# A hybrid encoder layer with experts: the first norm's gain and bias applied to turned tokens, 16 products for the residual rows inside the query projections, another order of VectorE's work in the last routing, and another order of the first expert pair's fetches

## The chip, the cores and the metric

The kernel runs on one core of one Trainium2 chip. Its time is the device time of one execution in microseconds (us); a median over several executions stands for a kernel. A profiled execution also has a span, from the first to the last recorded instruction. PE is TensorE (matmuls), DVE is VectorE, ACT is ScalarE, POOL is GpSimd, and SP is SyncE, which here only starts transfers (DMAs). Each engine carries out its own instructions strictly in order and waits on semaphores for the others.

## The reference, cut to what matters

512 tokens of 1024 features go through a layer norm, two attentions that read one input projection, a second norm, and a layer of 32 experts of which each token uses two.

```
h  = layer_norm(x, ln_emb_g, ln_emb_b)            # (x - mean) * rsqrt(var + eps) * g + b
p  = h @ w_in                                     # queries and keys of A, low-rank q and kv of B
A  = windowed attention of 8 heads, B = latent attention (q = rms(q_a) @ w_q_b, kv = rms(kv_a) @ w_kv_b)
h2 = layer_norm(alpha * h + concat(rms(A), rms(B)) @ w_out, ln_attn_g, ln_attn_b)
expert group: top 1 of 4; inside it the top 2 of 8 experts
y[t] = sum over t's two experts of w * ((silu(h2 @ w_gate[e]) * (h2 @ w_up[e])) @ w_down[e])
out = layer_norm(alpha * h2 + y, ...)
```

The first norm's result h is used twice: turned (features on the partitions) as the projections' operand, and as token rows `z` that are added to the attention's output much later.

## The kernel before, in words

The tokens are four tiles of 128 (`NT` = 4), the features eight blocks of 128 (`NK` = 8). Products that need more than one pass of TensorE's fp32 arithmetic are split into a high and a low part, and `mm3` makes three matmuls of one (high by high, low by high, high by low: the three lines 213 to 215). `split` makes the two parts: a copy on ScalarE (line 208) and a difference on VectorE or, for the first weight chunk's `wl`, on GpSimd (line 209).

1. **First norm** (the loop at lines 246 to 262). For each tile the rows are loaded, normalised with gain and bias by VectorE (lines 203 and 204), turned by TensorE (line 257), and split into `hth` and `htl`. The gain and the bias stand as rows repeated on all partitions (`lng`, `lnb`, four loads of 256 KB), and `cst`, which has the unit matrix for the turning, is loaded behind them on SP's queue. The first weights of `w_in` follow.
2. **Projections** by chunks of `w_in`, then the small projections of attention B: `wprep` loads, scales and splits pieces of `w_kv_b` and `w_q_b` (lines 358 to 360), `heads` turns keys and queries (line 468), lines 445 and 447 turn attention A's queries, and line 484 writes the values `vb`.
3. **Attentions B and A**, then the output projection.
4. **Routing.** For each token tile the logits of 36 outputs, the top expert group, and a place for each (token, expert). The last two tiles are called `a` (tile 2) and `b` (tile 3). From here on the order of all engines is the order of the code, written out by hand; up to here a scheduler with a model of the engines' times sets the order of every engine.
5. **Experts**, 16 pairs. The rows of a pair's tokens come by an indirect load from `norm_rows` (`fetch`, on GpSimd's queue), except for pair 0, whose rows `xT0` are made by matmuls with a one-hot matrix `sel` (`gather`, line 1109). A pair is 32 gate and up matmuls (`gates`, line 1243), the SiLU on ScalarE (1247), the product `hid` on VectorE (1248), and 16 matmuls with `w_dn` (1263). The weights of three pairs stand in a ring of buffers, loaded by SP in order: 4 MB for gate and up and 2 MB for down of each pair. A buffer is loaded anew as soon as its last reader is done.

In `run_pair` for pair 0 the kernel before issues four gate matmuls, then the 16 small matmuls that give the places of the next tokens (line 1368), `places_rows` and `fetch` for them, the mixing `weights` of tiles 1 to 3, and then the remaining gate matmuls. The gate matmuls go through the feature blocks 0 to 7.

Of the kernel before, what the change touches and what calls it, by code (L numbers as in the profile page):

```python
# [12 lines left out]
F32 = mybir.dt.float32  # L13
# [4 lines left out]
AF = mybir.ActivationFunctionType  # L18
# [3 lines left out]
P = 128  # L22
# [49 lines left out]
def build(tc, A, out):  # L72
# [24 lines left out]
    with top:  # L97
# [38 lines left out]
        def bvec(pl, src, n, name):  # L136
            t = pl.tile([P, n], F32, name=name)
            SY.dma_start(out=t, in_=src.partition_broadcast(P))
            return t
        load_x(0)  # L140
        lg, lb = [lp.tile([P, D], F32, name=nm) for nm in ("lng", "lnb")]
        for n in range(2):
            for dst, nm in ((lg, "ln_emb_g"), (lb, "ln_emb_b")):
                SY.dma_start(out=dst[:, 512 * n:512 * n + 512], in_=A[nm][512 * n:512 * n + 512].partition_broadcast(P))
        SY.dma_start(out=cst, in_=A["cst"][:, :C_KEEP])

        nch = [-1]

        def chunk_load(pieces):
            nch[0] += 1  # L150

            n = sum(w for _, w in pieces)
            hs = []
            for q in range(4):
                if q == 1 and nch[0] == 0:
                    load_x(1)
                wf, wh, wl = [wp.tile([P, 2, 512], dt, name=nm, bufs=4)
                              for nm, dt in (("wf", F32), ("wh", F32R), ("wl", F32R))]
                o = 0
                for c0, w in pieces:  # L160
                    SY.dma_start(out=wf[:, :, o:o + w],
                                 in_=A["w_in"][0, 256 * q:256 * q + 256, c0:c0 + w]
                                 .rearrange("(k p) f -> p k f", p=P))
                    o += w
                split(wf[:, :, :n], wh[:, :, :n], wl[:, :, :n], PO if nch[0] == 0 else V)
                hs.append((wh, wl))
            return n, hs
# [21 lines left out]
        def ln_stats(src, eps=LN_EPS):  # L189
# [7 lines left out]
            return mv, rs  # L197

        def layer_norm(src, dst, g, b):
            mv, rs = ln_stats(src)  # L200
            for i in range(2):
                sl = slice(512 * i, 512 * i + 512)
                V.scalar_tensor_tensor(dst[:, sl], src[:, sl], mv[:, 0:1], g[:, sl], ALU.subtract, ALU.mult)
                V.scalar_tensor_tensor(dst[:, sl], dst[:, sl], rs, b[:, sl], ALU.mult, ALU.add)

# [42 lines left out]
        for t in range(NT):  # L248
            if t == 0:
                chunks.append(chunk_load([(768, 512)]))  # L250
            elif t + 1 < NT:
                load_x(t + 1)
            layer_norm(xs[t], z[t], lg, lb)
            for kk in range(2):
                pt = ptr()
                for k in range(4):
                    PE.transpose(pt[:, k * P:(k + 1) * P],
                                 z[t][:, (4 * kk + k) * P:(4 * kk + k + 1) * P], ident)
                pv = pt.rearrange("p (a b) -> p a b", a=4)
                o = (slice(None), slice(4 * kk, 4 * kk + 4), slice(t * P, (t + 1) * P))  # L260
                split(pv, hth[o], htl[o])
        lnst.close()
# [199 lines left out]
        w2 = pool(p2, "w2", side="right")  # L462
        scr = pool(p2, "p2s", bufs=2, side="right")

        def heads(src, hi, lo, c, t):
# [21 lines left out]
        for c in range(2):  # L487
            wh, wl = wprep(w2, A["w_q_b"][0], gq, 6, 384 * c, 384)
            for t in range(NT):
                ts_ = slice(t * P, (t + 1) * P)  # L490
                qt_ = scr.tile([P, 4, 96], F32, name="qtok")
                pp = pproj()
                for k in range(6):
                    mm3(pp[:, :384], cth[:, k, ts_], ctl[:, k, ts_], wh[:, k, :], wl[:, k, :],
                        k == 0, k == 5)
                pv = pp[:, :384].rearrange("p (a b) -> p a b", a=4)
                SC.mul(qt_[:, :, 0:64], pv[:, :, 0:64], rq[t][:, 0:1])
                rope(qt_[:, :, 64:96], pv[:, :, 64:96], tabb, t, 4, 16, scr, scale=rq[t][:, 0:1])
                heads(qt_, qth, qtl, c, t)
# [648 lines left out]
        rsqrt(rr, sp[0][:, 0:1], ALPHA ** 2 / 512, ALPHA ** 2 * RMS_EPS)  # L1148
        norm_bias(a, 0)
        logits(a, 0)  # L1150
        logits(a, 1)
# [10 lines left out]
        wout_l(1, p1_)  # L1162
        steps(route(a))
        place(1)
        turn(b, 0)
        count(a)
        add_z(1, p1_)
# [9 lines left out]
        turn(b, 1)  # L1177
        place(a)
        sel0_(1)
        sel0_(a)  # L1180
        logits(b, 0)
        logits(b, 1)
        offset(b)
        for i in (1, 0):
            scaled(b, i)
        norm_gain(a, 1)
        biased(b)
        norm_bias(a, 1)
        for i in range(2):
            keep(a, i)  # L1190
        gather(0, range(2))
        gather(1, range(2))
        steps(route(b))
        count(b)
        gather(a, [0])
        gain(b, 1, V)
        place(b)
        sel0_(b)
        gather(a, [1])
        gain(b, 0, V)  # L1200
        shift(b, 1, V)
        shift(b, 0, V)
# [36 lines left out]

        def gates(pg, xT, ws, j0, j1):  # L1240
            for j in range(j0, j1):
                for i in range(2):
                    PE.matmul(pg[64 * i:64 * i + 64], xT[:, j, 64 * i:64 * i + 64], ws[i][0][j], start=(j == 0), stop=(j == 7))  # L1243

# [116 lines left out]
        def run_pair(p, xT, meanwhile):  # L1361
            pg = new_gates()
            if p == 0:
                gates(pg, xT, ws[p], 0, 2)
                pi = psd("places")
                for t in range(NT):
                    for u in range(4):
                        PE.matmul(pi[:, 2 * u:2 * u + 2], (sel0[t], sels[1][t])[u // 2][:, P * (u % 2):P * (u % 2) + P],
                                  cmb[t][:, 2 * u:2 * u + 2, 0], start=(t == 0 and u == 0), stop=(t == NT - 1 and u == 3))
                for g in range(2):  # L1370
                    for u, pl in enumerate(places_rows(pi[:, 4 * g:4 * g + 4], 2, 2, 1)):
                        plc[2 * g + u] = pl
                        fetch(2 * g + u, pl)
                for t in range(1, NT):
                    weights(t)
                gates(pg, xT, ws[p], 2, 8)
            else:
                gates(pg, xT, ws[p], 0, 8)
            load_next(p)
# [4 lines left out]
        def residual(p):  # L1384

            SC.mul(plc[p]["xg"], plc[p]["xg"], plc[p]["of"])

        xT = xT0
# [54 lines left out]
        with tc.If(nmax > 0):  # L1443
            with tc.For_i(0, NP) as p_:
# [3 lines left out]
                with tc.For_i(0, more) as r_:  # L1448
# [19 lines left out]
                    pg = new_gates("pwo")  # L1468
                    gates(pg, xT2, w_, 0, 8)
                    leave_rows(gated(pg), w_, pl)  # L1470
# [16 lines left out]
        with tc.issue_after(last):  # L1487
            gates(pg, xT, ws[p], 0, 8)
        hT = gated(pg)
# [121 lines left out]
```

## Time and profile before

| what | value |
|---|---|
| median of 3 runs | 592.62 us (591.76 to 593.85) |
| the profiled execution's own time | 591.33 us |
| its span | 589.5 us |
| PE busy | 523.4 us (89%) |
| DVE busy | 322.6 us (55%) |
| ACT busy | 222.1 us (38%) |
| POOL busy | 99.9 us (17%) |
| moved by DMA | 141.76 MB, mean 240 GB/s |

The rows further below are of two kinds. A row of a timeline gives the start, the length, the engine, the line, the operation, what it writes and reads, how many alike stand in the row, and in brackets how long the engine had been idle before it and what ended that. Where a row stands for several instructions, they overlap a little, so that the distance of two starts is shorter than one's length. A row of windows gives the busy time of each engine in a stretch, the granted TensorE clock as a part of 2.4 GHz, the DMA engines' busy share, and the GB/s.

### The profile page before, as it was taken

How to read it: one execution, taken by the hardware profiler on the slowest of the kernel's cores; microseconds unless marked ns; L12 is line 12 of the kernel's file. 1: busy time of each engine (PE TensorE's matmuls, PEld its weight loads, DVE VectorE, ACT ScalarE, POOL GpSimd, SP SyncE). 2: the span in 40 equal slices, each digit the busy share in tenths (PEclk: the TensorE clock that was granted, in tenths of full speed). 3: DMA queues.
4: the chain of work that ended last, by engine and by line, in shares of the span. 5: the costliest groups of instructions: out<-in, count | busy, mean ns of one | idle time of the engine just before them, and what ended most of it. 6: DMA issues, size and time to landing. Idle time of an engine off the chain costs nothing. (4 is left out here: it accounts for less than half of the span.)

```text
span 589.5 us, 8004 instructions
## 1 busy us (share of the span) xinstructions
PE 523.4 (89%) x2756; PEld 331.8 (56%) x2757; DVE 322.6 (55%) x882; ACT 222.1 (38%) x477; POOL 99.9 (17%) x141
## 2 busy tenths in 40 slices
PE   2899999999898999999998899999998699979860
PEld 1688898789766777677777444343433234323230
DVE  4946463775688757947768734434524222202177
ACT  2256451564597738856731312111111111101032
POOL 1700221311100000213200201123111101000051
PEclk9999999999899999999999989999999889989985
DMA  8983310221201005991266799999999999999663
GB/s 279 280 290 81 102 43 0 59 81 42 85 16 58 1 1 212 289 367 39 66 258 259 280 391 410 420 415 415 411 417 400 421 418 391 412 420 416 264 267 142
DMA packets 46268, 141.76 MB, mean 240 GB/s; under 512 B 12380, under 2 KB 19420, under 8 KB 37009
## 3 DMA queue, kind: packets, MB, share of 16 engines
q1 hardware_dynamic: 40608, 131.06, 58.5%
q0 software_dynamic: 4464, 8.06, 3.6%
q10 hardware_dynamic: 1152, 2.10, 0.9%
q8 instruction: 23, 0.38, 0.3%
q14 instruction: 21, 0.16, 0.1%
HBM read 133.14 MB, written 16.25 MB: 253 GB/s over the span
## 5 line engine op out<-in xcount | busy, mean ns | idle before, releaser
L1243 PE MATMUL p_gu<-w_gu,xT 128*64 128x512 f32 x512 | 125.0, 613 | 15.0 <-DMA w_gu<-in_w_gu 14.1
L1243 PEld LDWEIGHTS p_gu<-w_gu,xT 128*64 128x64 f32 x512 | 39.6, 141 | 95.6 <-issue 70.0
L1247 ACT ACTIVATE hid<-p_gu 128x256 f32<-128x256 f32 x16 | 6.1, 384 | 176.0 <-PE p_gu L1243 163.9
L1248 DVE TENSOR_TENSOR hid<-hid,p_gu 128x256 f32<-128x256 f32 x16 | 6.7, 421 | 113.9 <-ACT hid L1247 113.8
L1263 PE MATMUL p_y<-w_dn,hidT 128*64 128x512 f32 x256 | 59.9, 611 | 1.0 <-issue 0.6
L1276 DVE SCALAR_TENSOR_TENSOR xg<-p_y,wsl,xg 128x512 f32<-128x512 f32 x30 | 22.5, 751 | 28.4 <-PE p_y L1263 26.5
L1263 PEld LDWEIGHTS p_y<-w_dn,hidT 128*64 128x64 f32 x256 | 17.5, 140 | 31.4 <-issue 29.3
L604 PE MATMUL ptr<-cst,pr 128*128 128x128 f32 x208 | 33.3, 278 | 1.9 <-ACT pr L562 1.4
L1034 POOL DMA_INDIRECT xg<-norm_rows,tok x16 | 16.5, 1032 | 104.5 <-PE p_y L1263 16.8
L1269 POOL DMA_INDIRECT moe_rows<-xg,idx x15 | 15.6, 1039 | 95.0 <-DVE xg L1276 69.6
L604 PEld LDWEIGHTS ptr<-cst,pr 128*128 128x128 f32 x208 | 24.9, 145 | 9.5 <-ACT pr L562 3.2
L577 ACT ACTIVATE pr<-pmm,bnm 128x512 f32<-128x512 f32 x32 | 22.0, 689 | 10.6 <-DVE bnm L574 9.7
L574 DVE TENSOR_REDUCE bnm<-pmm 128x1 f32<-128x512 f32 x32 | 21.9, 687 | 5.3 <-PE pmm L215 4.8
L215 PE MATMUL pmm<-wh,htl 128*128 128x512 f32 (+1 forms) x64 | 24.0, 374 | 0.0
L213 PE MATMUL pmm<-wh,hth 128*128 128x512 f32 (+1 forms) x64 | 23.8, 372 | 0.0
L214 PE MATMUL pmm<-wl,hth 128*128 128x512 f32 (+1 forms) x64 | 23.5, 368 | 0.0
L562 ACT ACTIVATE pr<-pr,rc 128x512 f32<-128x512 f32 (+2 forms) x32 | 20.6, 645 | 4.1 <-DVE rc L560 3.9
L590 DVE CUSTOM_DVE_ANT_0 sm<-pmm,mask,nsink 128x256 f32<-128x256 f32 (+1 forms) x32 | 17.4, 545 | 7.6 <-PE pmm L587 6.5
L215 PE MATMUL pwo<-wh,htl 128*128 128x512 f32 (+1 forms) x56 | 20.7, 370 | 0.0
L214 PE MATMUL pwo<-wl,hth 128*128 128x512 f32 (+1 forms) x56 | 20.5, 367 | 0.0
L213 PE MATMUL pwo<-wh,hth 128*128 128x512 f32 (+1 forms) x56 | 20.5, 367 | 0.0
L1232 ACT ACTIVATE xg<-xg,of 128x1024 f32<-128x1024 f32 x15 | 17.2, 1149 | 8.5 <-PE p_x L1228 7.8
(349 smaller groups left out, 1161.6 us busy)
## 6 DMA issues: line engine op xcount, KB each, us to landing
w_gu<-in_w_gu SPq DMA_DIRECT2D x52, 1024.0 KB
w_dn<-in_w_dn SPq DMA_DIRECT2D x20, 1024.0 KB
w_gu<-in_w_gu SPq DMA_DIRECT2D x24, 512.0 KB
w_dn<-in_w_dn SPq DMA_DIRECT2D x24, 512.0 KB
wf<-in_w_in SPq DMA_DIRECT2D x12, 512.0 KB
moe_rows<-zr SPq DMA_DIRECT2D x8, 512.0 KB
rows<-moe_rows SPq DMA_DIRECT2D x8, 512.0 KB
wf<-in_w_q_b SPq DMA_DIRECT2D x12, 192.0 KB
```

What stands on the lines that cost most here:

```text
L213: PE.matmul(ps, ah, bh, start=first, stop=False)
L214: PE.matmul(ps, ah, bl, start=False, stop=False)
L215: PE.matmul(ps, al, bh, start=False, stop=last)
L562: SC.mul(pr[:, :n], pr[:, :n], rc)
L574: V.tensor_reduce(nm, sp, AX.X, ALU.max, negate=True)
L577: exps_.append(SC.activation(pr[:, :S], sp, AF.Exp, bias=nm, accum_out=den).ins)
L590: V.tensor_tensor_reduce(sm[:, :nk], sp[:, :nk], mask[:, mo:mo + nk], 1.0, nsink[:, h:h + 1], ALU.add, ALU.min, nm)
L604: PE.transpose(pt[:, k * P:(k + 1) * P], pr[:, k * P:(k + 1) * P], ident)
L1232: SC.mul(pl["xg"], pl["xg"], pl["of"])
L1243: PE.matmul(pg[64 * i:64 * i + 64], xT[:, j, 64 * i:64 * i + 64], ws[i][0][j], start=(j == 0), stop=(j == 7))
L1263: r = PE.matmul(py[64 * i:64 * i + 64, :], hT[:, j, 64 * i:64 * i + 64], ws[i][1][n][:, j], start=(j == 0), stop=(j == 1))
L1276: V.scalar_tensor_tensor(y, py, pl["wsl"], y, ALU.mult, ALU.add)
```

## The change

It has four parts.

1. The first norm's rows are made without gain and bias, by one ScalarE instruction for half a tile. After the turning a feature is a partition, so that gain and bias are one number per partition (`geT`): 128x128 pieces `hf` are made on VectorE, two in eight on ScalarE, and `hf` is split. The four loads of `lng` and `lnb` are gone. `cst` and `geT` are loaded from ScalarE's queue. The first chunk's `wl` are made by VectorE, no longer by GpSimd.
2. The token rows `z` now lack gain and bias, and get them inside the loop of the query projections: two VectorE instructions of 128x512 for each of eight halves, 16 in all, with the gain and the bias repeated on all partitions (`lgb`, two loads of 512 KB).
3. In the last routing, VectorE's order changes: tile `a`'s remaining norm stands earlier, `route(a)` is cut in two with `add_z(1)` between, and places, counts and gathers stand elsewhere.
4. In pair 0 the gate matmuls begin with blocks 4 to 7, and a function `first_rows` has the small matmuls, the `weights` of tile 1 before the places, and the fetches in the order 1, 0, 2, 3.

```diff
+        geT = cp.tile([P, 2, NK], F32, name="geT")
+        SC.dma_start(out=cst, in_=A["cst"][:, :C_KEEP])
+        SC.dma_start(out=geT, in_=A["ge_T"])
         load_x(0)
-        lg, lb = [lp.tile([P, D], F32, name=nm) for nm in ("lng", "lnb")]
-        for n in range(2):
-            for dst, nm in ((lg, "ln_emb_g"), (lb, "ln_emb_b")):
-                SY.dma_start(out=dst[:, 512 * n:512 * n + 512], in_=A[nm][512 * n:512 * n + 512].partition_broadcast(P))
-        SY.dma_start(out=cst, in_=A["cst"][:, :C_KEEP])
...
-                split(wf[:, :, :n], wh[:, :, :n], wl[:, :, :n], PO if nch[0] == 0 else V)
+                split(wf[:, :, :n], wh[:, :, :n], wl[:, :, :n])
...
-            layer_norm(xs[t], z[t], lg, lb)
+
+            mv, rs = ln_stats(xs[t])
+            nb = small.tile([P, 1], F32, name="ln_nb0")
+            V.scalar_tensor_tensor(nb, mv[:, 0:1], -1.0, rs, ALU.mult, ALU.mult)
             for kk in range(2):
+                sl = slice(512 * kk, 512 * kk + 512)
+                SC.activation(z[t][:, sl], xs[t][:, sl], AF.Identity, scale=rs, bias=nb)
                 pt = ptr()
...
-                pv = pt.rearrange("p (a b) -> p a b", a=4)
+                hf = lp.tile([P, 4, P], F32, name="hf", bufs=2)
+                for k in range(4):
+                    g_, b_ = [geT[:, i, 4 * kk + k:4 * kk + k + 1] for i in range(2)]
+                    if kk and k % 2:
+                        SC.activation(hf[:, k], pt[:, k * P:(k + 1) * P], AF.Identity, scale=g_, bias=b_)
+                    else:
+                        V.tensor_scalar(hf[:, k], pt[:, k * P:(k + 1) * P], g_, b_, ALU.mult, ALU.add)
                 o = (slice(None), slice(4 * kk, 4 * kk + 4), slice(t * P, (t + 1) * P))
-                split(pv, hth[o], htl[o])
+                split(hf, hth[o], htl[o])
...
+        lgb = [pool(p2, nm, side="right").tile([P, 2, 512], F32, name=nm) for nm in ("ln_emb_g", "ln_emb_b")]
+        for dst, nm in zip(lgb, ("ln_emb_g", "ln_emb_b")):
+            SY.dma_start(out=dst, in_=A[nm].rearrange("(a b) -> a b", a=2).partition_broadcast(P))
...
             for t in range(NT):
                 ts_ = slice(t * P, (t + 1) * P)
+
+                zt = z[t][:, 512 * c:512 * c + 512]
+                V.tensor_tensor(zt, zt, lgb[0][:, c], ALU.mult)
+                V.tensor_tensor(zt, zt, lgb[1][:, c], ALU.add)
...
         norm_bias(a, 0)
+        norm_gain(a, 1)
+        norm_bias(a, 1)
...
-        steps(route(a))
-        place(1)
+        ra = route(a)
+        steps(ra, 5)
         turn(b, 0)
-        count(a)
         add_z(1, p1_)
...
-                gates(pg, xT, ws[p], 0, 2)
...
-                for t in range(1, NT):
-                    weights(t)
-                gates(pg, xT, ws[p], 2, 8)
+
+                order = 4, 5, 6, 7, 0, 1, 2, 3
+                gates(pg, xT, ws[p], order, 0, 2)
+                first_rows()
+                gates(pg, xT, ws[p], order, 2)
...
+        def first_rows():
+
+            pi = psd("places")
+            for t in range(NT):
+                for u in range(4):
+                    PE.matmul(pi[:, 2 * u:2 * u + 2], (sel0[t], sels[1][t])[u // 2][:, P * (u % 2):P * (u % 2) + P],
+                              cmb[t][:, 2 * u:2 * u + 2, 0], start=(t == 0 and u == 0), stop=(t == NT - 1 and u == 3))
+            weights(1)
+            for g in range(2):
+                for u, pl in enumerate(places_rows(pi[:, 4 * g:4 * g + 4], 2, 2, 1)):
+                    plc[2 * g + u] = pl
+                for q in ((1, 0), (2, 3))[g]:
+                    fetch(q, plc[q])
+            for t in range(2, NT):
+                weights(t)
```

The 16 products of part 2 stand in the code inside the query loop, but the scheduler places them. This is VectorE's order there before, from the last piece of `w_kv_b` (`w2l`) through the low part of A's last queries (`qa`), the copies `q` of A's turned queries, and the first values `vb`:

```order
L360 SCALAR_TENSOR_TENSOR w2l<-wf_1262,gkv,w2h 128x512
L209 TENSOR_TENSOR qa_1147<-cqt,qa_1147 128x8x64
L447 CAST q_85<-ptr 128x512 x2
L484 TENSOR_SCALAR vb_1174<-pwo,rq_335 128x256
L484 TENSOR_SCALAR vb_1175<-pmm,rq_336 128x256
```

And this is the same place of VectorE's order in the changed kernel, where one of eight gain rows (line 499) and four of eight bias rows (line 500) are shown:

```order
L363 SCALAR_TENSOR_TENSOR w2l<-wf_1308,gkv,w2h 128x512
L499 TENSOR_TENSOR z_64<-z_64,ln_emb_g 128x512
...
L201 TENSOR_TENSOR qa_1183<-cqt,qa_1183 128x8x64
L500 TENSOR_TENSOR z_64<-z_64,ln_emb_b 128x512
L500 TENSOR_TENSOR z_65<-z_65,ln_emb_b 128x512
L500 TENSOR_TENSOR z_66<-z_66,ln_emb_b 128x512
L450 CAST q_85<-ptr 128x512
L500 TENSOR_TENSOR z_67<-z_67,ln_emb_b 128x512
...
L450 CAST q_85<-ptr 128x512
L490 TENSOR_SCALAR vb_1210<-pwo,rq_371 128x256
```

All eight gains stand between `w2l` and `qa`, three biases ahead of the first copy `q_85`, five between the two copies, and none behind them.

PE's order at the same place is the same in both kernels. These are its rows before, with the turning of A's last queries (line 445), of the keys `ktok` (line 468), and the next matmul of `w_kv_b`:

```order
L445 MATMUL ptr<-identr,qa_1100 128x128 x8
L445 MATMUL ptr<-identr,qa_1147 128x128 x8
L468 MATMUL ptr<-cst,ktok 96x128 x8
L213 MATMUL pwo<-w2h,cth 128x512
L214 MATMUL pwo<-w2l,cth 128x512
```

On SP's queue the two new loads stand between the pieces of `w_q_b` in the changed kernel:

```order
L361 DMA wf_1308<-in_w_kv_b 128x512
L361 DMA wf_1386<-in_w_q_b 128x384
L469 DMA ln_emb_g<-in_ln_emb_g 128x1024
L469 DMA ln_emb_b<-in_ln_emb_b 128x1024
L361 DMA wf_1390<-in_w_q_b 128x384
```

Before, the pieces of `w_q_b` follow one another there. The new loads write space that TensorE's last matmul with `hth` and `htl` leaves.

## Rows read from the trace of the kernel before

**Rows 1.** Windows over the stretches of the program, busy time of each engine.

```profile
25.00:100.00 75.00, 75.00 (x404) 64.27 (x403) 41.95 (x114) 34.56 (x74) 11.23 (x19) 1.00 0.38 123
114.00:118.00 4.00, 2.93 (x26) 2.57 (x25) 2.52 (x5) 2.15 (x5) 0.59 (x2) 1.00 0.00 0
118.00:154.00 36.00, 35.93 (x213) 33.66 (x212) 20.89 (x48) 17.51 (x35) 5.90 (x12) 1.00 0.18 51
154.00:162.00 8.00, 6.29 (x29) 4.85 (x28) 7.02 (x19) 5.50 (x14) 0.91 (x2) 0.79 0.53 155
162.00:303.00 141.00, 137.49 (x813) 101.66 (x811) 104.25 (x308) 97.69 (x249) 17.74 (x45) 1.00 0.36 129
330.00:338.00 8.00, 6.24 (x34) 2.49 (x33) 6.16 (x38) 0.85 (x2) 3.28 (x3) 1.00 0.64 186
338.00:344.00 6.00, 6.00 (x26) 2.55 (x24) 1.66 (x5) 0.68 (x1) 0.99 (x1) 0.72 1.00 378
344.00:449.00 105.00, 101.81 (x527) 42.22 (x526) 43.94 (x133) 18.59 (x26) 18.45 (x17) 1.00 1.01 412
449.00:557.00 108.00, 91.31 (x391) 32.97 (x390) 21.89 (x46) 13.18 (x19) 11.20 (x11) 0.95 0.98 398
```

**Rows 2.** Timeline of PE in the first 27 us.

```profile
10.53 1.95 PE L257 MATMUL ptr<-cst,z 128*128 128x128 f32 x8 [10.53 <-DMA cst<-cst]
13.23 1.22 PE L385 MATMUL pwo<-wh,hth 128*128 128x512 f32 x2 [0.76 <-ACT wh L208]
...
15.57 1.22 PE L385 MATMUL pwo<-wh,hth 128*128 128x512 f32 x2 [0.27 <-ACT wh L208]
...
19.75 1.09 PE L257 MATMUL ptr<-cst,z 128*128 128x128 f32 x4 [2.10 <-DVE z L204]
...
24.91 1.09 PE L385 MATMUL pwo<-wl,hth 128*128 128x512 f32 x4
```

**Rows 3.** Timeline of DVE in the same stretch.

```profile
3.49 0.69 DVE L192 BATCH_NORM_STATS2 ln_st<-xt 128x6 f32<-128x512 f32 x1 [2.46 <-DMA xt<-in_x]
...
16.77 5.61 DVE L204 SCALAR_TENSOR_TENSOR z<-z,ln_rs,lnb 128x512 f32<-128x512 f32 x2
```

**Rows 4.** Timeline of POOL in the same stretch.

```profile
16.57 8.05 POOL L209 TENSOR_TENSOR wl<-wf,wh 128x1024 fp32r<-128x1024 f32 x3
```

**Rows 5.** Timeline of PE where the query projections begin.

```profile
107.21 0.39 PE L215 MATMUL pmm<-wh,htl 128*128 128x512 f32 x1
...
115.00 0.84 PE L445 MATMUL ptr<-identr,qa 128*128 128x128 f32 x8 [0.54 <-DVE q L447]
...
117.18 0.48 PE L213 MATMUL pwo<-w2h,cth 128*128 128x512 f32 x1
```

**Rows 6.** Timeline of DVE at the same place.

```profile
110.72 1.18 DVE L360 SCALAR_TENSOR_TENSOR w2l<-wf,gkv,w2h 128x512 fp32r<-128x512 f32 x1
...
115.54 0.69 DVE L447 CAST q<-ptr 128x512 fp32r<-128x512 f32 x1 [0.69 <-PE ptr L445]
```

**Rows 7.** Timeline of POOL at the same place.

```profile
109.68 1.67 POOL L332 TENSOR_TENSOR cqt<-rp,rp 128x512 f32<-128x512 f32 x1 [1.25 <-DVE rp L329]
```

**Rows 8.** Timeline of DVE in the routing: products like those of part 2.

```profile
321.58 0.68 DVE L1122 TENSOR_TENSOR z<-z,lngb 128x512 f32<-128x512 f32 x1
...
323.34 1.28 DVE L1125 TENSOR_TENSOR z<-z,lngb 128x512 f32<-128x512 f32 x2
```

**Rows 9.** Timeline of PE: the waits ahead of the two stretches with a lowered clock.

```profile
156.47 0.50 PE L213 MATMUL pmm<-kth,qth 96*128 96x512 f32 x1 [1.71 <-ACT pr L577]
...
337.79 0.44 PE L1252 MATMUL p_t<-cst,hid 128*128 128x128 f32 x2 [1.76 <-DVE hid L1248]
```

**Rows 10.** Timeline of PE, ACT and DVE around pair 0.

```profile
326.92 1.94 PE L1243 MATMUL p_gu<-w_gu,xT 128*64 128x512 f32 x8 [0.78 <-DVE gn L892]
...
336.10 0.38 ACT L1247 ACTIVATE hid<-p_gu 128x256 f32<-128x256 f32 x1 [6.40 <-PE p_gu L1243]
...
337.32 0.42 DVE L1248 TENSOR_TENSOR hid<-hid,p_gu 128x256 f32<-128x256 f32 x1
```

More of the change, by code (lines that the diff above doesn't have):

```diff
@@ L197, in ln_stats @@
             return mv, rs
[L199 to L204, printed above, removed]
         def split(src, hi, lo, ev=None):
@@ L1177, in build @@
         turn(b, 1)
-        place(a)
+        steps(ra)
+        place(1)
         sel0_(1)
-        sel0_(a)
         logits(b, 0)
@@ L1185, in build @@
             scaled(b, i)
-        norm_gain(a, 1)
         biased(b)
-        norm_bias(a, 1)
         for i in range(2):
@@ L1191, in build @@
         gather(0, range(2))
+        count(a)
         gather(1, range(2))
         steps(route(b))
+        place(a)
+        sel0_(a)
         count(b)
-        gather(a, [0])
         gain(b, 1, V)
+        gather(a, [1])
         place(b)
         sel0_(b)
-        gather(a, [1])
+        gather(a, [0])
+        shift(b, 1, V)
         gain(b, 0, V)
-        shift(b, 1, V)
         shift(b, 0, V)
@@ L1238, in new_gates, with gates @@
             return ps.tile([P, 2 * FF], F32, name="p_gu", tag=tag, bufs=2)
-        def gates(pg, xT, ws, j0, j1):
-            for j in range(j0, j1):
+        def gates(pg, xT, ws, order=range(NK), n0=0, n1=NK):
+            for n in range(n0, n1):
+                j = order[n]
                 for i in range(2):
-                    PE.matmul(pg[64 * i:64 * i + 64], xT[:, j, 64 * i:64 * i + 64], ws[i][0][j], start=(j == 0), stop=(j == 7))
+                    PE.matmul(pg[64 * i:64 * i + 64], xT[:, j, 64 * i:64 * i + 64], ws[i][0][j], start=(n == 0), stop=(n == NK - 1))
         def gated(pg, meanwhile=lambda i: None):
@@ L1363, in run_pair @@
             if p == 0:
-                gates(pg, xT, ws[p], 0, 2)
[L1365 to L1373, printed above, removed]
-                for t in range(1, NT):
-                    weights(t)
-                gates(pg, xT, ws[p], 2, 8)
+                order = 4, 5, 6, 7, 0, 1, 2, 3
+                gates(pg, xT, ws[p], order, 0, 2)
+                first_rows()
+                gates(pg, xT, ws[p], order, 2)
             else:
-                gates(pg, xT, ws[p], 0, 8)
+                gates(pg, xT, ws[p])
             load_next(p)
@@ L1468, in build @@
                     pg = new_gates("pwo")
-                    gates(pg, xT2, w_, 0, 8)
+                    gates(pg, xT2, w_)
                     leave_rows(gated(pg), w_, pl)
@@ L1487, in build @@
         with tc.issue_after(last):
-            gates(pg, xT, ws[p], 0, 8)
+            gates(pg, xT, ws[p])
         hT = gated(pg)
@@ L1595 @@
     give("w_gu", np.concatenate([gate, up], axis=3).transpose(0, 2, 1, 3))
+    give("ge_T", np.stack([np.asarray(inputs[n]).reshape(NK, P).T for n in ("ln_emb_g", "ln_emb_b")], axis=1))
     give("gb_T", np.stack([np.asarray(inputs[n])[0].reshape(NK, P).T for n in ("ln_attn_g", "ln_attn_b")], axis=1))
```

## The prediction, made before the changed kernel had run

> **What bounds the kernel now.** I read the windows first [rows 1], to see in which stretches a later or earlier TensorE means a later or earlier end. From 25 to 100 TensorE is busy for all of 75 us, and from 118 to 154 for 35.93 of 36: there its work follows without gaps, nothing that comes late can be caught up, and what is won ahead of 25 us stays. The reader is to see three thinner places. From 114 to 118 it works 2.93 of 4 us. From 154 to 303, the attentions, 1.71 + 3.51 = 5.2 us are idle, and in the first 8 us the granted clock is 0.79, a loss of 0.21 x 8 = 1.7 us: 6.9 us in all. From 344 on the transfers bound the kernel: the DMA engines are full (share 1.01, 412 GB/s) while TensorE still works 101.81 of 105 us, and from 449 to 557 it waits for weights and works 91.31 of 108.
>
> Then I read the timelines at the places that the change touches, engine by engine. In the first 25 us TensorE waits for `cst` until 10.53, multiplies weights first at 13.23, and is held again at 19.75 by the norm of the second tile [rows 2]. VectorE waits 2.32 us for the repeated gain, and its two bias steps at 16.77 take 5.61 us [rows 3], beside GpSimd's splits [rows 4], where one such step takes some 0.75. At the query projections TensorE's next matmul of `w_kv_b` starts at 117.18, behind VectorE's second copy `q` at 115.54 [rows 5, 6].
>
> **Part 1, the first norm: 3.5 us won.** 1 MB of loads leaves the front of SP's queue, and `cst` no longer stands behind it, so the 10.53 us shrink [rows 2]. Two prices are to be had from the rows. The idle times at 15.57 and 19.75 make 0.27 + 2.10 = 2.4 us [rows 2]. And the pairs of matmuls of line 385 take 1.22 / 2 = 0.6 each or a little less, against 1.09 / 4 = 0.27 in the row at 24.91 [rows 2]; sixteen stand ahead of that row, and with 0.25 each they lose 4 us. Of these I count on less than half, 1.8 us, since TensorE comes from idle again and must work its way up to the full clock. Against this, VectorE has new work: four splits of 128x1024, 1.3 us each like two 128x512 products [rows 8], and six `hf` pieces for each tile, between 0.2 (a quarter of a 128x512 step of 0.69 [rows 3]) and 0.69. In its new order some 10 us of work (four statistics at 0.69, three splits, six pieces at 0.25, two `htl`, small ones) lie ahead of the first tile's last `htl`: from 3.49 on that is 13.5 without a wait, and with some 4 us of waits for weights 17.5, where the slow pairs end before. I let this take back 0.7. So 2.4 + 1.8 - 0.7 = 3.5, an estimate. The bounds are 1.0 (idle time alone, and twice the delay) and 5.5 (all of idle time, four fifths of the slow matmuls, no delay). Because TensorE is full to 100 us [rows 1], this gain stands in full at the query projections.
>
> **Part 2, the 16 products: 9.2 us lost.** The order shows where they stand: eight gains ahead of `qa`, three biases ahead of the first copy `q`, five ahead of the second. VectorE executes in order, so all 16 are done before the second copy, and TensorE's turning of the keys and the next matmul of `w_kv_b` wait for that copy. VectorE ends `w2l` at 110.72 + 1.18 = 111.9 [rows 6]. Two products of this size start 1.28 - 0.68 = 0.60 apart [rows 8], so 16 take 9.6, and `qa` and the first copy 0.65 each (0.69 long, like the copy in [rows 6], and overlapping a little): the second copy starts at 111.9 + 9.6 + 1.3 = 122.8 where it started at 115.54 [rows 6]. That is 7.3 us, and all of it reaches TensorE, which had waited 0.54 for the copies already [rows 5] and has nothing else in its queue until the copy is there.
>
> The gain rows must have landed by then. They write where the last matmul with `htl` has read, at 107.21 + 0.39 [rows 5]; the first x tile, 256 KB, was used at 3.49 [rows 3], that is at most 3.5 us after the program's start, and at 412 GB/s 256 KB more cost 0.6 us [rows 1]. So they are there at 107.6 + 3.5 + 0.6 = 111.7 or sooner, in time for 111.9; the bias rows are needed 5 us later. `w_q_b` behind them on SP's queue comes some 2.5 us later, which the block covers, because VectorE reaches those pieces only behind it.
>
> The wait has a second price. TensorE stands still from about 114.5 to 120 and again for some 2.5 us. After waits of 1.71 and 1.76 us [rows 9] the granted clock of the next stretches is 0.79 over 8 us and 0.72 over 6 us [rows 1], which is 0.21 x 8 = 1.7 and 0.28 x 6 = 1.7 us lost; the 0.54 us waits at 115 left it at 1.00 [rows 1, 5]. I take 1.9, one such stretch and a little for the second wait. The bounds are 0, if the clock stays, and 3.4, if both waits cost a stretch. So 7.3 + 1.9 = 9.2, between 7.3 and 10.7. From there to 154 TensorE is full [rows 1], and nothing catches this up.
>
> One thing could make the block longer. VectorE's steps at 16.77, which read two operands from SBUF, took 5.61 / 2 = 2.8 us beside GpSimd's splits [rows 3, 4], four times their usual time. GpSimd has a product of 1.67 us near the block [rows 7]. It ends at 111.35, before the block starts at 111.9, so I add nothing; if the two met, VectorE would wait at most these 1.7 us. The Trainium skill's page "SBUF — State Buffer", section "SBUF: two separate sides", gives the reason: an operation of VectorE with two SBUF inputs and a GpSimd operation that reads SBUF exclude each other for a whole instruction. By that rule the sum would be up to 1.7 us higher if they meet; rows 3 and 4 agree with it.
>
> **The attentions: 0 +- 3.** The scheduler orders them anew, because its model sees other times. It had 6.9 us of idle time and lowered clock there, and I have no row that says whether the new order has less.
>
> **Parts 3 and 4, the routing and pair 0: 0.7 us won.** Counted through VectorE's new order with the rows of before, the gate matmuls start about 2.3 us sooner than 326.92 and end about 2 us sooner than at 336.1, where SiLU follows them [rows 10]. `hid` came 0.8 us after SiLU had ended, since the `weights` stood ahead of it on VectorE (336.10 + 0.38 against 337.32); with the fetch chain sooner that wait goes, and perhaps the lowered clock of 338 to 344 too. But from 344 on the weight stream is the bound [rows 1]: what counts is when the loads of the ring start. They wait for pair 0's gates, buffer by buffer, in SP's order, and the first load waits for the buffer with blocks 0 and 1, which is now read last but two. From 330 to 338 the DMA engines are busy for 0.64 only [rows 1]. In that stretch the loads start 2 to 2.4 us sooner, but some 0.6 to 0.7 MB less has gone ahead, 1.6 us at 412 GB/s. The difference is 0.4 to 0.8; I take 0.7, with bounds of 2.2 won (no loss of early bytes) and 0.8 lost. VectorE's fetch order alone is hidden behind pair 0's gates.
>
> **The sum.** On the profiled execution: 591.33 + 9.2 - 3.5 + 0 - 0.7 = 596.3. That execution is 1.29 below the median of 592.62, so I predict 597.6 for the median, +0.8%. No difference below 0.3% (1.8 us) can be told from no change, so "faster" begins below 590.8 and "slower" above 594.4.
>
> **The rivals.**
> - *Cheap block, large first gain* (0.16): the clock stays up after the block, and the start gives 5.5. Then 592.6 + 7.3 - 5.5 - 0.7 = 593.7, no change. For it: the clock stood at 1.00 after the 0.54 us waits [rows 1, 5]. Against: these are a tenth of the wait expected here.
> - *The attention order*, the one on the other side (0.10): the new order removes the idle time and the lowered clock of 154 to 303, all 6.9 us. Then 597.6 - 6.9 = 590.7, faster. It decides from 6.8 us on. For it: both waits that started the slow stretch are short and depend on the order [rows 9]. Against: the same scheduler left them there, and a shift of TensorE by itself removes no wait of an engine for ScalarE's softmax.
> - *The first part does not do what it says* (0.09): VectorE, with splits and `hf`, is the new chain at the start, and TensorE is no earlier at 25 us. Then 597.6 + 3.5 = 601.1. For it: VectorE gets 4 x 1.3 us of splits and 24 pieces there. Against: the 5.61 us of [rows 3] were mostly waiting, which goes with GpSimd's splits [rows 4].
> - *The block meets GpSimd's product, or the gain rows come late* (0.09): 597.6 + 1.7 = 599.3.
>
> My forecast itself has 0.54, with a range of its own from 594.5 to 601; the remaining 0.02 I give to a faster result with two favourable bounds at once. So faster has 0.12, same 0.16, slower 0.72. The low end of the range takes in the first rival with the best bound of the routing (592.6 + 7.3 - 5.5 - 2.2 = 592.2), the high end the worst of the block and the start (592.6 + 10.7 - 1.0 = 602.3): 592.2 to 602.3. Outside are the second rival and a part of the third, under 0.2.
>
> **What the profile of the changed kernel would show.** Part 1: TensorE's first matmul on weights ahead of 13.2, and the row that now stands at 24.91 some 3 to 4 us sooner. Part 2: 16 rows of 0.68 us on VectorE in one block, TensorE's wait for a copy `q` of 5 us or more behind it, and a clock of 0.7 to 0.8 in the 6 to 8 us that follow; if the block lies there and TensorE doesn't wait, my main term is wrong. Attention: idle time and clock from the block's end to the routing, against 6.9 us. Pair 0: gates 2 us sooner relative to the routing's start, `hid` right behind SiLU, and the end moved by less than 1 us for it.

## The result, and the profile after

The changed kernel takes 602.0 us (median of 5, 599.34 to 603.37), the kernel before 592.67 (median of 5, 591.76 to 594.32). The ratio is 1.0146 with a 95% interval of 1.0111 to 1.0181: slower by 1.5%. The profiled execution of the changed kernel is the fastest of its five (599.34 us, span 597.7), that of before had 591.33 (span 589.5), so the two traces differ by 8.2 us of span.

Where these 8.2 us arise is read from one instruction at a time that both kernels have. The times of before stand in [rows 5], [rows 9] and [rows 10] or in the same timeline further on.

| TensorE or SP at | before | after | later by | since the row above |
|---|---|---|---|---|
| last matmul of the input projection | 107.21 | 104.66 | -2.55 | -2.55 |
| next matmul of `w_kv_b` behind A's last queries | 117.18 | 122.53 | +5.35 | +7.90 |
| first matmul with `w_q_b` | 124.56 | 131.35 | +6.79 | +1.44 |
| first scores of attention B | 153.37 | 160.16 | +6.79 | 0 |
| first turning of the last tile | 313.07 | 319.71 | +6.64 | -0.15 |
| first gate matmul of pair 0 | 326.92 | 331.34 | +4.42 | -2.22 |
| first gate matmul of pair 1 | 345.98 | 351.87 | +5.89 | +1.47 |
| load of the experts' result rows | 557.89 | 566.08 | +8.19 | +2.30 |
| end of the span | 589.5 | 597.7 | +8.2 | 0 |

The block of 16 products is the second row. This is VectorE's timeline there in the changed kernel:

```profile
108.17 1.18 DVE L363 SCALAR_TENSOR_TENSOR w2l<-wf,gkv,w2h 128x512 fp32r<-128x512 f32 x1
110.15 4.91 DVE L499 TENSOR_TENSOR z<-z,ln_emb_g 128x512 f32<-128x512 f32 x8 [0.80 <-DMA ln_emb_g<-in_ln_emb_g]
114.97 0.68 DVE L201 TENSOR_TENSOR qa<-cqt,qa 128x512 fp32r<-128x512 f32 x1
115.57 1.89 DVE L500 TENSOR_TENSOR z<-z,ln_emb_b 128x512 f32<-128x512 f32 x3
117.38 0.68 DVE L450 CAST q<-ptr 128x512 fp32r<-128x512 f32 x1
117.98 3.09 DVE L500 TENSOR_TENSOR z<-z,ln_emb_b 128x512 f32<-128x512 f32 x5
120.99 0.68 DVE L450 CAST q<-ptr 128x512 fp32r<-128x512 f32 x1
```

And this is TensorE's timeline at the same place, with its four waits and the slow matmuls behind them:

```profile
111.12 0.80 PE L448 MATMUL ptr<-identr,qa 128*128 128x128 f32 x8
115.80 0.72 PE L448 MATMUL ptr<-identr,qa 128*128 128x128 f32 x4 [3.88 <-DVE qa L201]
118.12 0.75 PE L448 MATMUL ptr<-identr,qa 128*128 128x128 f32 x4 [1.60 <-DVE q L450]
119.63 1.06 PE L474 MATMUL ptr<-cst,ktok 128*96 128x128 f32 x4 [0.77 <-ACT q L450]
121.82 1.06 PE L474 MATMUL ptr<-cst,ktok 128*96 128x128 f32 x4 [1.12 <-DVE q L450]
122.53 0.78 PE L205 MATMUL pwo<-w2h,cth 128*128 128x512 f32 x1
123.11 0.63 PE L206 MATMUL pwo<-w2l,cth 128*128 128x512 f32 x1
```

The waits add up to 3.88 + 1.60 + 0.77 + 1.12 = 7.4 us, where before there were two of 0.54 [rows 5]. From 122.53 on the matmuls stand 0.43 apart instead of 0.23. The windows show the same as a clock; the last column but two is the granted clock:

```profile
111.00:122.00 11.00, 3.63 (x23) 2.67 (x22) 11.00 (x20) 2.12 (x4) 0.36 (x1) 0.70 0.07 22
122.00:126.00 4.00, 4.00 (x13) 3.26 (x13) 2.52 (x6) 0.95 (x2) 0.29 (x1) 0.54 0.00 0
126.00:158.00 32.00, 31.93 (x191) 29.99 (x190) 18.50 (x42) 16.15 (x32) 4.34 (x9) 1.00 0.19 57
```

VectorE is busy for all of 11 us, TensorE for 3.63; then TensorE works at 0.54 of its clock; and from 126 on it is full, so that nothing is caught up.

In the first norm, TensorE's rows that answer to [rows 2] are these:

```profile
9.22 1.97 PE L254 MATMUL ptr<-cst,z 128*128 128x128 f32 x8 [9.22 <-ACT z L251]
13.05 1.22 PE L388 MATMUL pwo<-wh,hth 128*128 128x512 f32 x2 [1.85 <-ACT hth L200]
15.13 1.22 PE L388 MATMUL pwo<-wh,htl 128*128 128x512 f32 x2 [0.87 <-DVE htl L201]
...
21.53 1.98 PE L388 MATMUL pwo<-wl,hth 128*128 128x512 f32 x8
```

The first matmul on weights is hardly sooner (13.05 against 13.23), because it now waits for the added step `hf` and its split; the gain comes behind 17 us, where the wait for the second tile's norm is gone and the clock rises sooner: the row with `wl` stands at 21.53 instead of 24.91, and the first matmul of the second tile at 23.34 instead of 25.84.

Around pair 0 the rows that answer to [rows 10], and those of ScalarE and GpSimd that matter now, are:

```profile
331.34 1.94 PE L1256 MATMUL p_gu<-w_gu,xT 128*64 128x512 f32 x8
...
335.71 5.37 PE L1256 MATMUL p_gu<-w_gu,xT 128*64 128x512 f32 x24
...
351.87 3.65 PE L1256 MATMUL p_gu<-w_gu,xT 128*64 128x512 f32 x16 [1.33 <-ACT xT L1241]
```

```profile
339.68 1.27 POOL L1044 DMA_INDIRECT xg<-norm_rows,tok  x1 [17.24 <-DVE wc L921]
341.26 1.01 POOL L1044 DMA_INDIRECT xg<-norm_rows,tok  x1 [0.31 <-DVE wc L921]
```

```profile
350.20 1.15 ACT L1391 ACTIVATE xg<-xg,of 128x1024 f32<-128x1024 f32 x1 [8.66 <-DMA xg<-norm_rows,tok]
351.25 0.56 ACT L1241 COPY xT<-p_x 128x512 f32<-128x512 f32 x1
```

The first fetch now brings the rows of the next pair, the second those that pair 0's `residual` multiplies. The second is issued at 341.26 and its user starts at 350.20. The copy of `xT` for pair 1 stands behind it on ScalarE, and TensorE waits 1.33 us for that copy. Before, the same ScalarE step waited 1.04 us and stood at 337.53.

SP's first load into the ring behind pair 0's gates also comes later, at 339.39 (before: 328.88), and the DMA engines are nearly idle just ahead of it; the last column is GB/s:

```profile
337.00:339.00 2.00, 2.00 (x12) 0.72 (x10) 1.76 (x15) 0.00 (x0) 0.00 (x0) 1.00 0.10 39
339.00:341.00 2.00, 2.00 (x10) 0.43 (x6) 1.78 (x10) 0.00 (x0) 1.27 (x1) 1.00 0.32 53
```

### The profile page after: what moved, and what is told of

Read it like the earlier page. It is cut to its first block, busy times and chain, and to the rows that moved or that the text cites. A ratio compares the mean times of both kernels' runs of the same rounds, so it can differ in the third digit from the quotient of the medians.

```text
span 597.7 us, 8038 instructions
## 1 busy us (share of the span) xinstructions
PE 525.9 (88%) x2756; PEld 331.1 (55%) x2757; DVE 331.2 (55%) x914; ACT 231.6 (39%) x493; POOL 88.6 (15%) x137
## 5 line engine op out<-in xcount | busy, mean ns | idle before, releaser
L1256 PEld LDWEIGHTS p_gu<-w_gu,xT 128*64 128x64 f32 x512 | 38.4, 140 | 99.7 <-issue 71.2
L1044 POOL DMA_INDIRECT xg<-norm_rows,tok x16 | 16.5, 1030 | 102.1 <-issue 23.5
## 6 DMA issues: line engine op xcount, KB each, us to landing
w_dn<-in_w_dn SPq DMA_DIRECT2D x24, 512.0 KB, 13.8
```

## The experiments

Twelve kernels, each timed beside the kernel before, whose median in these comparisons was 593.9 to 594.3; so I go by ratios. Edits refer to the changed kernel unless they say "before", and `...` stands for lines that are not shown.

**1. No products.** The computation lacks the residual rows' gain and bias here.

```diff
...
-            SY.dma_start(out=dst, in_=A[nm].rearrange("(a b) -> a b", a=2).partition_broadcast(P))
...
-                V.tensor_tensor(zt, zt, lgb[0][:, c], ALU.mult)
-                V.tensor_tensor(zt, zt, lgb[1][:, c], ALU.add)
```

> The changed kernel without the 16 products and without the loads of their two operands (part of the computation is left out: the residual rows lack gain and bias). Theory A, the block holds TensorE: the wait of 7.9 us and the lowered clock of some 1.6 us go, TensorE's first matmul behind A's last queries stands near 115 instead of 122.5, and the time falls by 8 to 10 us, to 592 to 594. Rival B, the loss comes from other places (the attentions' new order, the routing, pair 0) and the block is mostly hidden: the time stays above 598.

Measured: 592.07 us, ratio 0.9958 (0.9935 to 0.9982). TensorE's timeline is back to two short waits, and the next matmul of `w_kv_b` stands at 114.95:

```profile
112.77 0.84 PE L448 MATMUL ptr<-identr,qa 128*128 128x128 f32 x8 [0.54 <-DVE q L450]
114.15 1.05 PE L471 MATMUL ptr<-cst,ktok 128*96 128x128 f32 x8 [0.54 <-DVE q L450]
114.95 0.48 PE L205 MATMUL pwo<-w2h,cth 128*128 128x512 f32 x1
```

Against the changed kernel's ratio of 1.0146 that is 0.0188, about 11 us, with some 2.5 to either side if the two intervals are combined. The 7.90 + 1.44 = 9.3 us that the block and the clock behind it cost in the trace lie inside that. The block accounts for all of the loss and more. Theory A holds.

**2. The products spread behind the query heads.**

```diff
...
-                V.tensor_tensor(zt, zt, lgb[0][:, c], ALU.mult)
-                V.tensor_tensor(zt, zt, lgb[1][:, c], ALU.add)
...
-                heads(qt_, qth, qtl, c, t)
+                mark = heads(qt_, qth, qtl, c, t)
+                zt = z[t][:, 512 * c:512 * c + 512]
+                with tc.issue_after(mark):
+                    V.tensor_tensor(zt, zt, lgb[0][:, c], ALU.mult)
+                    V.tensor_tensor(zt, zt, lgb[1][:, c], ALU.add)
```

> The changed kernel with the 16 products tied behind the query heads, two behind each, so that none stands ahead of the copies of A's last queries; all is computed. Theory A: it is the place and not the work that costs, so the time is that of the kernel without products within 1 us, 592 to 594. Rival C: VectorE's 9.6 us of work cost wherever they stand in the projections, because the query heads wait for VectorE there: 596 or more.

Measured: 596.3 us, ratio 1.0049 (1.0030 to 1.0068). Some 5.4 us of the 11 come back in another place. TensorE no longer waits at A's queries, but at the start of attention B, for the first softmax:

```profile
144.88 0.64 PE L474 MATMUL ptr<-cst,qtok 128*96 128x128 f32 x4 [0.30 <-POOL qtok L335]
...
154.92 0.53 PE L205 MATMUL pmm<-kth,qth 96*128 96x512 f32 x1 [2.26 <-ACT pr L589]
...
164.24 0.50 PE L205 MATMUL pmm<-kth,qth 96*128 96x512 f32 x1 [0.77 <-ACT pr L589]
```

Run 1 has one wait there, of 1.71 us, so these three make 1.6 us more; and from 152 to 164 the granted clock is 0.72 on average, where run 1 has 0.86, which is worth up to 1.7 us more. The rest of the 5.4 us I have not placed. So the place is not all: at the end of the projections VectorE has no 9.6 us to spare either, as rival C says. The time lies 2.3 us above the upper end of theory A.

**3 and 4. Parts 1 and 2 alone; parts 3 and 4 alone.** The edits are the parts of the diff as they stand.

> Parts 1 and 2 alone, with the routing and pair 0 of before. Theory A and D, pair 0's later weight loads cost some 1.6 us: 599.5 to 601, a little faster than the changed kernel. My forecast's step, parts 3 and 4 win 0.7: 602.5 to 603.

> Parts 3 and 4 alone, on the kernel before. Theory D, the gates start 2 us sooner but the ring's loads wait for the buffer that is now read last but two: 593.5 to 595, slower than before by 1 to 2 us, with SP's first load of the third pair ahead some 8 us later than the gates' start. My forecast's step: 592.0, 0.7 us faster.

Measured: parts 1 and 2, 601.03 us, ratio 1.0131 (1.0105 to 1.0157); parts 3 and 4, 595.5 us, ratio 1.0022 (0.9994 to 1.0051). Parts 1 and 2 make nearly all of the loss: run 3 stands at the upper end of theory D, and its distance from the changed kernel, 0.0015, is within the intervals. Parts 3 and 4 win nothing, though the gates start sooner; a loss of 1.3 us is likely but not beyond the interval. SP's first load in run 4 comes 9.7 us behind the gates' start (338.91 against 329.21), where before it comes 2.0 us behind it.

**5. The products on GpSimd in attention B** (part 1, with the routing and pair 0 of before). The operands are loaded in halves, since there is room for no more.

```diff
...
+        for c in range(2):
+            gb_ = lg_load(c)
+            for t in range(NT):
+                zt = z[t][:, 512 * c:512 * c + 512]
+                PO.tensor_tensor(zt, zt, gb_[0], ALU.mult)
+                PO.tensor_tensor(zt, zt, gb_[1], ALU.add)
```

> Part 1 alone, with the 16 products on GpSimd at the start of attention B (their operands in halves, loaded there), routing and pair 0 of before; all is computed. Theory A: part 1 is worth 2.5 us once nothing waits for the products, so 590.5 to 592, some 2 us faster than before. Rival E: GpSimd's products, which read two operands from SBUF, stop VectorE's work of the same kind in the attention as they did in the first norm: TensorE's first wait in attention B grows and the time is 594 or more.

Measured: 596.73 us, ratio 1.0039 (1.0008 to 1.0070), so rival E by the time, and 0.0101 or some 6 us above the same kernel with the products earlier (run 9). The groups of VectorE's lines from 150 to 220 show it; the columns are count, busy time, mean ns of one, and the idle time ahead. First with the products on GpSimd, then before:

```profile
L575 DVE TENSOR_SCALAR pr<-pr,rc 128x512 f32<-128x512 f32 x14 | 9.2, 656 | 0.2
...
L536 DVE SCALAR_TENSOR_TENSOR wobl<-wfo,gob,wobh 128x1024 fp32r<-128x1024 f32 x4 | 7.9, 1982 | 0.0
```

```profile
L564 DVE TENSOR_SCALAR pr<-pr,rc 128x512 f32<-128x512 f32 x14 | 6.7, 482 | 0.2
...
L525 DVE SCALAR_TENSOR_TENSOR wobl<-wfo,gob,wobh 128x1024 fp32r<-128x1024 f32 x4 | 5.1, 1280 | 0.5 <-ACT wobh L524 0.5
```

The same instructions take 656 instead of 482 ns and 1982 instead of 1280, while those that read PSUM keep their time (683 and 687 ns for the row maximum). TensorE's first wait in attention B does not grow, as E had it: it is 1.71 us as before. What is new are three later waits for VectorE's `pr`, of 0.94, 1.01 and 2.48 us at 170.03, 177.14 and 183.25.

**6. The products on VectorE inside attention B**, two behind a unit's row maximum (otherwise as in run 5).

```diff
...
+                zt = z[t][:, 512 * c:512 * c + 512]
+                with tc.issue_after(nms_[-1]):
+                    V.tensor_tensor(zt, zt, lgc[0][0], ALU.mult)
+                    V.tensor_tensor(zt, zt, lgc[0][1], ALU.add)
```

> The same with the products on VectorE, two behind a unit's row maximum, from the fifth unit of attention B on. Theory A: 590.5 to 592.5. Rival C, VectorE is the chain there too and 9.6 us of work cost 3 or more: 594 and above.

Measured: 595.35 us, ratio 1.0019 (0.9987 to 1.0051): C, some 4.8 us above the same kernel with the products earlier (run 9), though not clear of the kernel before. VectorE is busy for all of 160 to 180 there, and TensorE's busy time from 170 to 180, which is 9.11 us in the trace of before, falls to 7.67:

```profile
160.00:170.00 10.00, 9.01 (x50) 5.51 (x48) 10.00 (x23) 7.05 (x17) 0.00 (x0) 1.00 0.11 38
170.00:180.00 10.00, 7.67 (x41) 4.29 (x39) 10.00 (x20) 6.99 (x15) 0.00 (x0) 1.00 0.26 71
```

**7. Parts 3 and 4 with the gates in the order 0 to 7.**

```diff
-                order = 4, 5, 6, 7, 0, 1, 2, 3
+                order = range(NK)
```

> Parts 3 and 4 alone with the gate matmuls in the order 0 to 7. Theory D, the order of the gates costs because the first buffer of the ring comes free last: SP's first load of the third pair ahead starts 2 us behind the gates' start again, the stretch from the gates' start to the end goes from 266.5 back to about 263 us, and the time is 2 us or more below that of parts 3 and 4 with the turned order, about 591.5. Rival F, the loss comes from the fetches (later rows, a residual that ScalarE waits for): no change against parts 3 and 4, 595.

Measured: 593.63 us, ratio 0.9995 (0.9965 to 1.0026), against 1.0022 with the turned order. SP's first load stands at 327.60 with the gates' start at 325.64, so the later first load that theory D names does come from the turned order. But the stretch from the gates' start to the end is 266.1 us, not 263, and ScalarE still waits 8.1 us for the fetched rows: D's number fails, and F is not excluded. In TensorE's timeline the wait for `xT` is then 2.39 us:

```profile
344.93 8.78 PE L1246 MATMUL p_gu<-w_gu,xT 128*64 128x512 f32 x32 [2.39 <-ACT xT L1231]
```

**8. The kernel before, with the first chunk's low parts on VectorE.**

```diff
-                split(wf[:, :, :n], wh[:, :, :n], wl[:, :, :n], PO if nch[0] == 0 else V)
+                split(wf[:, :, :n], wh[:, :, :n], wl[:, :, :n])
```

> The kernel before with one change: the first chunk's four low parts are made by VectorE instead of GpSimd. If GpSimd's splits stop VectorE's steps at 16.77, these take 1.4 instead of 5.6 us, the second tile's turning stands about 1 to 3 us sooner than 19.75, and the time falls by 1 to 2 us. Rival: VectorE's new work of 5 us takes the place of the wait, and the time stays within 0.5 us.

Measured: 592.55 us, ratio 0.9958 (0.9926 to 0.9990): faster by 0.4% from one argument. The bias steps of the second tile, 5.61 us for two in [rows 3], are:

```profile
18.44 0.74 DVE L204 SCALAR_TENSOR_TENSOR z<-z,ln_rs,lnb 128x512 f32<-128x512 f32 x1
...
19.71 0.74 DVE L204 SCALAR_TENSOR_TENSOR z<-z,ln_rs,lnb 128x512 f32<-128x512 f32 x1
```

They take 0.74 each. The turning of the second tile stands at 20.69, not sooner than 19.75, against what I expected: the scheduler put it behind the matmuls with `wl`, which now run at 19.30. The last matmul of the input projection stands at 105.59, 1.6 us sooner than before, of the 2.55 that the whole of part 1 gives.

**9. Part 1 with the products during the second chunk of the projections**, their operands in a buffer of the weights' ring; routing and pair 0 of before.

```diff
+        def lg_load(c):
+            r = wp.tile([P, 2, 512], F32, name="wf", bufs=4)
+            for i, nm in enumerate(("ln_emb_g", "ln_emb_b")):
+                SY.dma_start(out=r[:, i], in_=A[nm][512 * c:512 * c + 512].partition_broadcast(P))
+            return r[:, 0], r[:, 1]
...
+            if t % 2 == 0:
+                lg_ = lg_load(t // 2)
+            for u in range(2):
+                rows(2 * (t % 2) + u, t // 2, lg_, m_)
```

> Part 1 with the 16 products on VectorE during the second chunk of the projections (some 45 to 65 us), where TensorE is full and VectorE idle for nearly half; their operands use a buffer of the weights' ring; routing and pair 0 of before; all is computed. Theory A: the 2.5 to 3 us of the first norm reach the end, so 590.5 to 591.5 against 594 for the kernel before here, ratio 0.994 to 0.996. Rival G, the new orders that the scheduler makes of the attentions eat the gain whatever the products do: ratio 1.000 or more.

Measured: 590.38 us, ratio 0.9938 (0.9915 to 0.9960): theory A, and faster than both kernels. The 16 products stand between 53.8 and 71.8. VectorE's busy time from 25 to 100 grows from 41.95 [rows 1] to 49.75, and TensorE stays full:

```profile
25.00:100.00 75.00, 74.45 (x401) 63.70 (x400) 49.75 (x132) 39.14 (x83) 14.05 (x18) 1.00 0.36 117
```

**10 and 11. The same with parts 3 and 4**, the gates in the order 0 to 7 (10), and turned as in the changed kernel (11).

> The same with parts 3 and 4, the gate matmuls in the order 0 to 7. Theory D: the same ratio as with the routing of before within 0.002, since the weight stream and not the gates' start sets the end.

> The same with parts 3 and 4 as in the changed kernel, the gate matmuls in the order 4 to 7, 0 to 3. Theory D: 1.5 us or more slower than with the order 0 to 7, and the DMA engines nearly idle (under 50 GB/s) for 2 us some 18 to 20 us after the last tile's turning, where the other order has over 200. Rival F: no difference between the two orders.

Measured: order 0 to 7, 589.93 us, ratio 0.9927 (0.9901 to 0.9953); turned, 590.82 us, ratio 0.9943 (0.9917 to 0.9969). Run 11 differs from the changed kernel only in the place of the 16 products and of their operands: 0.9943 against 1.0146 is 0.0203, some 12 us, for the same work at another place. The intervals of 9, 10 and 11 overlap widely. The idle DMA engines belong to the turned order, as theory D says: in its trace they move 1 GB/s from 18 to 20 us behind the last tile's turning, with the order 0 to 7 254 in the same stretch. Theory D's price for it, 1.5 us or more, is not shown: the two ratios differ by 0.0016, about 1 us, within their intervals. In both TensorE waits for `xT` ahead of pair 1's gates, 2.15 us (turned) and 2.55 us.

**12. Part 3 alone on the kernel before.**

> Part 3 alone on the kernel before: VectorE's order in the last routing. If it wins by itself, the gates start 1.5 to 2.2 us sooner behind the last tile's turning, and the end comes 0 to 1 us sooner (stream-bound), ratio 0.998 to 1.000. Rival: it costs, because the rows for the next pairs are written and fetched later: ratio above 1.001 and a wait of ScalarE for the first fetched rows above 1.0 us.

Measured: 591.31 us, ratio 0.9974 (0.9946 to 1.0003). The gates start 12.5 us behind the first turning of the last tile instead of 13.85, and TensorE doesn't wait for `xT`. ScalarE waits 5.29 us for the fetched rows, more than the rival's 1.0, but this does not reach the end as the rival had it. VectorE's order in the routing by itself is more likely a gain than a loss; the interval ends just above 1. Part 4 on top of it gave 1.0022 (run 4): the difference is 0.0048, with about 0.004 to either side if the two intervals are combined, so part 4 takes the gain back.

The fourteen traces show where. The table has two stretches for each: from the first turning of the last tile to the first gate matmul of pair 0, and from there to the end of the span.

| routing and pair 0 | traces | turning to gates | gates to end |
|---|---|---|---|
| as before | before, runs 3, 5, 6, 8, 9 | 13.8 to 16.5 | 262.4 to 263.6 |
| part 3 | run 12 | 12.5 | 262.7 |
| parts 3 and 4, order 0 to 7 | runs 7, 10 | 12.5 | 266.1, 264.9 |
| parts 3 and 4, turned | changed kernel, runs 1, 2, 4, 11 | 11.6 | 265.4 to 267.3 |

In run 12 part 3 starts the gates sooner at no cost behind them. With part 4 the stretch behind is 2.2 to 4.6 us longer than in run 12, and it is longer in the order 0 to 7 already; the turned order lengthens it by about as much (0.9 us in the mean) as it starts the gates sooner.

## Why the prediction was right, and where its terms were off

- **The main term was right**: 16 products ahead of the second copy `q`, read from the order, hold TensorE. I had 7.3 us; measured are 7.9. The difference is the wait of 0.80 us for the gain rows: I had them land at 111.7 or sooner in the time of before, in time for VectorE; they landed at 110.15 in the changed kernel's time, 4.8 us after their issue at 105.38, and not 3.5 plus 0.6. That is the second half of the fourth rival, at 0.80 us of its 1.7. GpSimd's product, the first half, ended at 108.80, ahead of the block. So the Trainium skill's rule on GpSimd and VectorE ("SBUF — State Buffer", section "SBUF: two separate sides") did not apply here. It does apply in the first norm (run 8) and in attention B (run 5), where the steps with two SBUF operands took 5.61 us for two instead of 0.74 each, and 1982 instead of 1280 ns: the traces agree with it.
- **The lowered clock** was 1.9 us in the forecast and 1.44 in the table.
- **The first norm** gave 2.55 us where I had 3.5. The step that was mis-sized is VectorE's new work: with `hf` and its split the first weights' matmuls wait 1.85 and 0.87 us, where before they waited 0.76 and 0.27; that is more than the 0.7 that I took back.
- **The attentions**: -0.15 where I had 0.
- **Routing and pair 0** is the term whose mechanism failed. The gates' start came 2.22 us sooner, as forecast (2.3). But I had the ring's loads start 2 to 2.4 us sooner too, at a price of 1.6 us of lost early bytes; the first load comes 8.05 us behind the gates' start (339.39 against 331.34) instead of 1.96, which is 3.9 us later relative to the routing, and the DMA engines stand nearly idle ahead of it. The sentence "VectorE's fetch order alone is hidden behind pair 0's gates" does not hold in this trace: the swapped fetches put pair 0's own rows second, these are there 8.9 us after their issue instead of 3.7, and ScalarE, with `xT` behind them, is late for pair 1. In runs 1, 2 and 4, with the same part 4, they take 5.2 to 5.7 us and TensorE does not wait for `xT`; what makes the difference is not shown. From the gates' start to the end the changed kernel takes 266.4 us and before 262.6, so the 2.2 us are more than lost.
- **The size and sign of this term** are less sure than the mechanism. Between the two traces the end comes 1.55 us later relative to the routing (8.19 - 6.64), where I had 0.7 sooner; but the trace of before has nearly the shortest way to the gates of its six (13.85 us of 13.8 to 16.5). The ratios show no gain, and a loss only within their intervals (runs 3 and 4). By run 12 against run 4 part 4 costs about what part 3 gains. By the table above the larger piece of part 4 is not the turned order but the fetches or the earlier `weights` of tile 1, from two traces against one; these two were not tried by themselves.
- The sum on the profiled execution was 596.3; it took 599.34. By terms: block +0.6, clock -0.5, first norm +0.95, attentions -0.15, routing and pair 0 +2.25, together +3.2; the difference is 3.0. The median is another 2.7 above the profiled execution, more than the 1.29 that I had added from before. So the loss is nearly twice the forecast (1.5% against 0.8%), the median lies 0.3 us below the top of the range and outside my forecast's own 594.5 to 601: the direction and the main cause were read, but that the range held the time was in part luck.

Of the rivals only that half of the fourth came true, and it is too small to decide. The clock did fall behind the block (0.54), TensorE was ahead by 2.5 us at 25 us, and the attentions took as long as before within 0.15 us.

## What to carry to other kernels

An instruction that is cheap and free in time is not free in place. Where a scheduler places it, look up what stands behind it on its engine, and whether the bounding engine waits for that; here 9.6 us of VectorE's work cost some 11 us at one place (run 1), about 5 us at two others (run 2 against 1, run 6 against 9), and nothing measurable where TensorE was full and VectorE half idle (run 11 against 1). Given to GpSimd in attention B it cost some 6 us (run 5 against 9). That of several rows fetched in turn the one should go first whose user has the busiest queue behind it is a guess: no run tried the order of the fetches by itself.

## What the runs showed of the hardware that was not expected

TensorE's granted clock does not fall behind every wait of the same length. Run 4 has the same order as before up to the routing, and the same wait of 1.71 us for the first softmax (at 156.69, in [rows 9] at 156.47). These are the windows of before and then of run 4; the clock is the last column but two:

```profile
150.00:160.00 10.00, 8.29 (x45) 7.17 (x44) 6.75 (x21) 4.32 (x11) 2.57 (x6) 0.89 0.40 115
160.00:170.00 10.00, 10.00 (x57) 7.02 (x57) 7.49 (x19) 8.87 (x21) 0.00 (x0) 0.94 0.03 10
...
180.00:190.00 10.00, 8.41 (x47) 5.58 (x48) 8.23 (x19) 8.69 (x22) 0.00 (x0) 1.00 0.01 3
```

```profile
150.00:160.00 10.00, 8.09 (x47) 6.88 (x46) 6.85 (x21) 4.78 (x11) 2.56 (x6) 1.00 0.36 104
160.00:170.00 10.00, 9.90 (x59) 6.79 (x58) 7.80 (x21) 8.73 (x21) 0.00 (x0) 1.00 0.05 21
...
180.00:190.00 10.00, 8.63 (x38) 5.31 (x39) 7.23 (x16) 7.65 (x19) 0.00 (x0) 0.83 0.00 1
```

Before, the clock falls right behind the wait; in run 4 it stays at 1.00 there and falls some 25 us later, behind waits of 1.07 and 1.17 us at 180.20 and 183.17. Before has these too, of 0.92 and 1.17 us at 180.42 and 183.39, and its clock stays at 1.00 behind them. Just ahead of the last routing, from 310 to 316, run 4's granted clock is 0.50, the lower of its two levels, where before has 1.00; the nearest longer wait ahead of it is one of 0.29 us at 306.73, and before has one of 0.28 at 305.38. So two profiled executions of nearly the same order differ by several us (the last tile's first turning stands at 317.57 in run 4 and 313.07 before), and I let the ratios decide.

GpSimd's work beside VectorE costs VectorE a good part of what it relieves it of. In the first norm two steps of 0.74 us took 5.61 beside GpSimd's splits, 4.1 us more ([rows 3], run 8), and the four splits take VectorE 4.8 us when it makes them itself (run 8). In attention B the two groups of run 5 take 5.3 us more, against 9.6 us of products.
